# A two-layer hybrid decoder trunk on one core: its list scheduler gets other priorities, another order of tiles and chunks, and other places for the modulation weights in the weight stream

## The chip, the cores and the metric

The kernel runs on one core of a Trainium2 chip. The metric is the device time of one execution in microseconds (us), lower is better. Times are medians of several executions. One further execution was recorded with the hardware profiler, and every duration below comes from that record.

The engines are called as the profile calls them: PE is the matrix unit (its weight loads are listed apart as PEld), DVE the vector engine, ACT the scalar engine, POOL the general one, SP the one that issues most DMAs. Each engine works through its own instructions strictly in the order in which the program gives them; between engines only semaphores set the order.

## What is computed

```python
for l in range(2):
    shift, scale, gate = split(c @ w_ada[l] + b_ada[l], 3)         # adaLN, from one row c
    u = x * (1 + scale) + shift                                    # x is 256 x 1024
    h = u @ w_in[l]                                                # 1024 -> 4032 columns, cut among groups
    o = concat[DSA(4 heads), FoX(6 heads), NSA(6 heads)]           # three kinds of attention
    x = LayerNorm(ALPHA * x + (1 + gate) * ((o * silu(h["gate"])) @ w_out[l]))
```

- **DSA** scores all earlier tokens with a small indexer (8 heads of 32), keeps the 64 best of each row (top-k) and attends to those alone.
- **FoX** is causal attention with a decay that is summed over the tokens.
- **NSA** adds up a compressed, a selected and a windowed branch, each weighted by a gate. With 256 tokens the selected and the windowed branch are both plain causal attention here.

All inputs are float32.

## The kernel before, in words

**Matmuls.** A float32 product of the big projections is made of three passes over reduced floats: each weight piece is cast to a high part (ACT, L516, `wh`) and the remainder is taken by a subtraction (DVE, L534, `wl`); the function `mm3` (L549 to L551) then issues high x high, low x high and high x low. Every weight piece of 512 KB therefore costs a DMA (`raw`), a cast on ACT, a subtraction on DVE, and matmuls. Six `raw` buffers and five `wh` buffers exist.

**Modulation.** The adaLN product `c @ w_ada` is a row times a matrix and is done on DVE: one `scalar_tensor_tensor` with a row sum for each 128 x 1024 piece (L583), 24 pieces for each layer. Such a piece also goes through a `raw` buffer. Its key in the stream is `("ada", layer, j, h)`; h = 0, 1 are scale and shift, needed before the layer starts, h = 2 is the gate, needed at its end.

**Stages of a layer.** (1) Four *chunks* A, B, C, D of about 450 to 512 columns each are projected with tokens on the partitions, for two token halves t = 0, 1: A holds the indexer's queries and keys, B the DSA queries and keys, C the NSA keys, D the NSA queries; the values are spread over all four. After a chunk ACT copies it out (`chunk`), DVE rotates it (rope, L641 to L644), PE transposes it (L655) and ACT copies the transposes. (2) Sixteen *tiles* of 128 columns are projected with columns on the partitions (24 matmuls each): tiles 0 and 1 feed the compressed branch, tiles 2 to 7 are key and query of the three FoX pairs, tiles 8 to 15 are the eight blocks of the output gate. (3) Among the tiles run 11 *pair steps* of attention (two heads at a time: 3 NSA pairs twice, 3 FoX, 2 DSA). Each is a chain over all engines: scores on PE (L722, with L727, L730 or L732 for decay and masks), row maxima on DVE (L677), exponentials on ACT (L681), reciprocal sums on DVE (L667, L668, L670), normalisation on ACT (L694), transposes on PE (L704), a copy on ACT (L708), values on PE (L753), and a copy of the result on ACT (L975). (4) Block i of the output gate times block i of the attention result gives `mH`, `mL` (L1136 to L1141). (5) The output projection takes four pieces for each of two column halves; piece q needs gate blocks 2q and 2q+1. Then residual, LayerNorm, and for layer 0 the next layer's `u` (L1379, L1389, L1403, `uL` L1407) and the affine part of the LayerNorm on x itself (L1430).

DSA's mask comes from the top-k: eight rounds of a maximum and a replacement on DVE (L925, L926) for each token half, after the indexer (L906, L911, L886).

**What sets the order.** Nothing of this is written out by hand. Each piece of work is a generator that asks for an engine and a modelled duration, and a list scheduler (class `Order`) emits instructions in the order of its own modelled clock. On each engine it takes, of what is ready, the task with the lowest priority number. Two things steer it, and both lie in the table `PR` (L364): the priority numbers (`nsa0`, `dsa1`, `fox1` and so on; the last digit is the layer), and the lists that write the weight stream:

```python
        for c in PR["cord"]:
            chunk(c, l)
...
        a, b = PR["ada_at"]
        extra += [(a + b * j, [("ada", 1, j, h) for h in range(2)]) for j in range(8)]
...
        for i in range(16):
            tiles(l, pr("tord", l)[i])
```

`ada_at = (a, b)` puts the pieces of step j of the next layer's scale and shift behind the stream position a + b*j, counted in tiles. SP issues the stream in this order, each DMA as soon as a `raw` buffer is given back. `acc` is the number of PSUM banks that projections may hold, and `aff` the priority of the affine step L1430.

Of the kernel before, what the change touches and what calls it, by code (L numbers as in the profile page):

```python
# [179 lines left out]
def stream_order():  # L180
    o = []

    def chunk(c, l):
        o.extend((c, l, q) for q in range(4))
# [10 lines left out]
    for l in range(DEPTH):  # L195
# [10 lines left out]
        else:  # L206
            for c in PR["cord"]:
                chunk(c, l)
        extra = []
        if l == 0:  # L210
            a, b = PR["ada_at"]
            extra += [(a + b * j, [("ada", 1, j, h) for h in range(2)]) for j in range(8)]
        a, b = PR["adag_at"][l]
        extra += [(a + b * j, [("ada", l, 2 * j + i, 2) for i in range(2)]) for j in range(4)]
# [18 lines left out]
class Order:  # L233
# [38 lines left out]
    def _unblock(self):  # L272
        moved = True
        while moved:
            moved = False
            for t in sorted(self.tasks, key=self._key):
# [6 lines left out]
                elif r[0] == "R":  # L283
# [3 lines left out]
                    if cls in ("s", "pt", "o", "ms", "ad"):  # L287
                        side = sum(self.used.get((tag, c), 0) for c in ("s", "pt", "o", "ms", "ad"))
                        if side + n > PR["side"]:
                            continue  # L290
# [19 lines left out]
    def run(self):  # L310
        while True:
            self._unblock()
            best = None
            for e in "PAVG":
                cand = [(t["ready"] + self.LAT[e], t) for t in self.tasks if t["req"][0] == e]
                if not cand:
                    continue
                first = max(self.free_at[e], min(r for r, _ in cand))
                r, t = min((z for z in cand if z[0] <= first + (PR["tol"] if self._key(z[1])[0] <= -2 else 0.02)),
                           key=lambda z: self._key(z[1]))  # L320
# [14 lines left out]
def pr(name, l):  # L335
    return PR.get(f"{name}{l}", PR.get(name))

# [23 lines left out]


RW = [6, 5]
PR = dict(zn='VV', upart=4, ul='VVVV', nrm='AAAA', cord='ABDC', t1q=0, cuts=(0, 512, 1024), oq=(0, 1, 2, 3), tord=(0, 1, 2, 3, 4, 5, 6, 7, 8, 9, 10, 11, 12, 13, 14, 15), gpp=(0, 1), res=-3.5, warm=10, tol=0.1, ada_at=(12, 0.25), adag_at=((0, 0.5), (11, 1)), ow=(512, 256), aff=0, tw=512, nact=((0, 0), (1, 0), (0, 1), (1, 1)), pro='', gp0=(0, 1), gp1=(0, 1), acc=4, s=2, pt=1, o=3, ms=3, side=8, topk=3, idx=2, dec=0.5, cmp=1.2, nsa=1.6, dsa=1.7, fox=1.8, gate=4, gate1=6, ada=6, main=10, ev=0, split=4, nahead=2, acc1=1.5, cmp1=3, dec0=1.45, nsa1=1.6, topk1=6, nsa0=1.3, dec1=0.5, idx1=0.3, tord1=(2, 3, 4, 5, 6, 7, 0, 1, 8, 9, 10, 11, 12, 13, 14, 15), dsa0=1.4, oq0=(1, 0, 2, 3), cmp0=1.2, fox1=1.5, dsa1=1.7, fox0=1.1, oq1=(1, 2, 3, 0), topk0=3, tord0=(0, 1, 2, 3, 4, 5, 6, 7, 8, 9, 10, 11, 12, 13, 14, 15), idx0=2, nrm1='AAAA', nrm0='AAAA', t1q0=0, t1q1=0)  # L364


@with_exitstack
# [1117 lines left out]
```

## Time and profile before

| | us |
|---|---|
| median of 3 runs | 391.98 (390.94 to 393.09) |
| the profiled execution | 391.34 |
| its span (first to last instruction) | 389.6 |

| stage, by the stream of PE's work | from, us | to, us |
|---|---|---|
| layer 0: chunks with the modulation | 0 | 61 |
| layer 0: ropes, first indexer and NSA scores | 61 | 80 |
| layer 0: tiles and pairs | 80 | 177 |
| layer 0: output projection | 177 | 198 |
| LayerNorm, next `u`, first chunk of layer 1 | 198 | 217 |
| layer 1: rest of the chunks | 217 | 262 |
| layer 1: tiles and pairs | 262 | 362 |
| layer 1: output projection | 362 | 380 |
| last LayerNorm and output | 380 | 389.6 |

A row of the stage view gives a stretch of time, its length, then for PE, PEld, DVE, ACT and POOL the busy time in it with the number of instructions, then PE's granted clock as a share of full speed, the DMA engines' busy share and GB/s. A row of the timeline gives start and duration in us, engine, line, operation, output<-input, shapes, a count where equal instructions are merged, and in brackets the idle time of that engine just before and who ended it.

### The profile page before, as it was taken

Reading aid. Unit: us, or ns where it says so; the run is one execution under the profiler, and the core shown is the slowest. Engines: PE = TensorE matmul, PEld = TensorE weight load, DVE = VectorE, ACT = ScalarE, POOL = GpSimd, SP = SyncE. Lnnn points to the kernel's source line nnn. Section 1 sums busy time; section 2 is a strip of 40 time slices with the busy share of each in tenths; the row PEclk is TensorE's granted clock in tenths of the full one; section 3 lists DMA queues with packets and bytes.
Section 4 is the critical chain, followed back from the end, with each engine's and each line's share of the span. In section 5 each row is a group of like instructions: output and inputs, shape, how many; then the busy total and the mean of one; then the engine's idle time right before and its main releaser. Section 6 shows DMA issues by size and latency. Waiting matters only on the chain.

```text
span 389.6 us, 6872 instructions
## 1 busy us (share of the span) xinstructions
PE 352.2 (90%) x2430; PEld 284.8 (73%) x2430; DVE 314.6 (81%) x766; ACT 252.6 (65%) x664; POOL 8.1 (2%) x14
## 2 busy tenths in 40 slices
PE   5899999799999998589977999999999999997990
PEld 1687788588886786377956768878888898864790
DVE  5798879998989998978899889999565688553766
ACT  3564458676996868773385656556998646987520
POOL 2000000000000000000000000000000000000014
PEclk9899999999999999979988999999999999998996
DMA  7999997638425658796644554563355695110002
GB/s 228 411 408 397 360 352 305 217 110 303 130 64 177 194 177 297 245 315 209 216 133 172 145 174 115 163 209 108 110 142 187 170 407 179 48 63 0 1 2 108
DMA packets 22074, 75.47 MB, mean 194 GB/s; under 512 B 2964, under 2 KB 3096, under 8 KB 21912
## 3 DMA queue, kind: packets, MB, share of 16 engines
q1 hardware_dynamic: 21752, 74.75, 57.1%
q8 instruction: 19, 0.31, 0.3%
q10 hardware_dynamic: 288, 0.29, 0.2%
q14 instruction: 15, 0.12, 0.1%
HBM read 73.98 MB, written 1.05 MB: 193 GB/s over the span
## 4 chain that ended last, share of the span: by engine, by line
PE 49%; DVE 26%; DMA 12%; ACT 8%; issue 4%; DVEq 0%; SPq 0%; ACTq 0%
DMA raw<-in_wst_dram 12%; PE b L549 11%; PE b L551 11%; PE b L550 10%; DVE wl L534 6%; PE b L722 4%; PE b L753 3%; PE b L704 3%; DVE raw L583 2%; DVE iacc L926 2%; DVE iacc L886 2%; ACT wh L516 2%; ACT p L694 2%; DVE m L925 2%; DVE roped L641 1%
## 5 line engine op out<-in xcount | busy, mean ns | idle before, releaser
L516 ACT CAST wh<-raw 128x1024 fp32r<-128x1024 f32 (+2 forms) x81 | 83.3, 1030 | 55.7 <-DMA raw<-in_wst_dram 28.4
L534 DVE TENSOR_TENSOR wl<-raw,wh 128x1024 fp32r<-128x1024 f32 (+2 forms) x81 | 96.2, 1193 | 13.7 <-ACT wh L516 12.9
L549 PE MATMUL b<-uH,wh 128*128 128x256 f32 x256 | 77.4, 302 | 0.0
L551 PE MATMUL b<-uH,wl 128*128 128x256 f32 x256 | 72.9, 285 | 0.2 <-DVE wl L534 0.2
L550 PE MATMUL b<-uL,wh 128*128 128x256 f32 x256 | 72.7, 284 | 0.0
L583 DVE SCALAR_TENSOR_TENSOR raw<-raw,cbc 128x1024 f32<-128x1024 f32 x48 | 58.0, 1218 | 4.3 <-DMA raw<-in_wst_dram 4.0
L549 PE MATMUL b<-wh,uH 128*128 128x512 f32 (+1 forms) x128 | 52.4, 410 | 3.0 <-ACT uH L1359 2.3
L551 PE MATMUL b<-wh,uL 128*128 128x512 f32 (+1 forms) x128 | 51.5, 402 | 3.3 <-DVE uL L1407 1.6
L549 PEld LDWEIGHTS b<-uH,wh 128*128 128x128 f32 x256 | 49.2, 192 | 2.4 <-issue 1.5
L550 PE MATMUL b<-wl,uH 128*128 128x512 f32 (+1 forms) x128 | 51.0, 398 | 0.0
L551 PEld LDWEIGHTS b<-uH,wl 128*128 128x128 f32 x256 | 49.2, 192 | 0.6 <-DVE wl L534 0.6
L550 PEld LDWEIGHTS b<-uL,wh 128*128 128x128 f32 x256 | 49.3, 193 | 0.1
L681 ACT ACTIVATE p<-b,nmx 128x128 f32<-128x128 f32 x88 | 36.3, 428 | 3.5 <-DVE nmx L677 3.4
L694 ACT ACTIVATE p<-p,rinv 128x128 f32<-128x128 f32 (+1 forms) x88 | 33.8, 451 | 2.8 <-DVE rinv L668 1.4
L551 PEld LDWEIGHTS b<-wh,uL 128*128 128x128 f32 x128 | 25.1, 196 | 10.6 <-DVE uL L1361 3.9
L704 PE MATMUL b<-cf,p 128*128 128x128 f32 x132 | 23.9, 290 | 9.4 <-ACT p L694 9.4
L549 PE MATMUL b<-wh,mH 128*128 128x256 f32 (+1 forms) x96 | 31.9, 332 | 0.5 <-ACT mH L1139 0.5
L551 PE MATMUL b<-wh,mL 128*128 128x256 f32 (+1 forms) x96 | 31.2, 325 | 0.5 <-DVE mL L1141 0.5
L549 PEld LDWEIGHTS b<-wh,uH 128*128 128x128 f32 x128 | 25.2, 197 | 8.8 <-ACT uH L1359 2.8
L550 PE MATMUL b<-wl,mH 128*128 128x256 f32 (+1 forms) x96 | 31.1, 324 | 0.0
L708 ACT COPY pT<-b 128x384 f32<-128x384 f32 x44 | 21.2, 484 | 11.6 <-PE b L704 11.1
L550 PEld LDWEIGHTS b<-wl,uH 128*128 128x128 f32 x128 | 24.9, 194 | 4.1
(174 smaller groups left out, 565.0 us busy)
## 6 DMA issues: line engine op xcount, KB each, us to landing
raw<-in_wst_dram SPq DMA_DIRECT2D x120, 512.0 KB, 4.6
raw<-in_wst_dram SPq DMA_DIRECT2D x7, 480.0 KB, 6.6
lnr<-in_lnrow_dram SPq DMA_DIRECT2D x4, 512.0 KB, 4.9
raw<-in_wst_dram SPq DMA_DIRECT2D x4, 448.0 KB, 4.1
xT_sb<-in_xT_dram SPq DMA_DIRECT2D x4, 256.0 KB, 6.6
x_sb<-in_x_dram SPq DMA_DIRECT2D x1, 1024.0 KB, 7.7
out_dram<-x_sb SPq DMA_DIRECT2D x3, 256.0 KB, 2.2
cf<-in_cst_dram SPq DMA_DIRECT2D x1, 384.0 KB
```

What stands on the lines that cost most here:

```text
L516: A.copy(h[:, :n], loaded[key])
L534: V.tensor_tensor(lo[:, :n], raw, h[:, :n].bitcast(F32), op=ALU.subtract)
L549: T.matmul(o, ah, bh, start=start, stop=False)
L550: T.matmul(o, ah, bl, start=False, stop=False)
L551: T.matmul(o, al, bh, start=False, stop=stop)
L583: V.scalar_tensor_tensor(w, w, 1.0, cbc, op0=ALU.mult, op1=ALU.mult, accum_out=mods[l][:, j, h:h + 1])
L681: A.activation(p_sb[:, P * t:P * t + P * (t + 1)], so[:, P * t:P * t + P * (t + 1)], AF.Exp, bias=nmx[:, t, a:a + 1], accum_out=st[:, t, a ...
L694: A.mul(blk, blk, r[:, t, a:a + 1])
L704: T.transpose(pt[:, i, :], p_sb[:, P * i:P * i + P], ident)
L708: A.copy(pT, pt.rearrange("p a b -> p (a b)"))
L722: T.matmul(sp[a][:, P * t:P * t + nk], qT[r, t * P:(t + 1) * P], kT[r, :nk], start=True, stop=False, skip_group_check=True)
L753: T.matmul(O[64 * a:64 * a + 64, P * kt:], vs(a, kt), outs[a][0][:, 256 * kt:256 + 128 * kt], start=(first and kt == 0), stop=(last and kt ...
```

## The change

One line changes, the table `PR`. Its changed entries, one to a line:

```diff
-cord='ABDC'   ada_at=(12, 0.25)   adag_at=((0, 0.5), (11, 1))   aff=0   acc=4
+cord='DCAB'   ada_at=(10, 0.5)    adag_at=((0, 0.5), (8, 1))    aff=0.49   acc=5
...
-dec0=1.45  dsa0=1.4   cmp0=1.2   fox0=1.1
+dec0=0.28  dsa0=0.12  cmp0=1.39  fox0=1.48
-tord0=(0, 1, 2, 3, 4, 5, 6, 7, 8, 9, 10, 11, 12, 13, 14, 15)
+tord0=(0, 1, 3, 4, 5, 6, 7, 8, 9, 10, 11, 12, 13, 2, 14, 15)
...
-nsa1=1.6   topk1=6    idx1=0.3   fox1=1.5   dsa1=1.7   oq1=(1, 2, 3, 0)
+nsa1=5.08  topk1=5.9  idx1=0.64  fox1=1.95  dsa1=4.17  oq1=(1, 3, 2, 0)
-tord1=(2, 3, 4, 5, 6, 7, 0, 1, 8, 9, 10, 11, 12, 13, 14, 15)
+tord1=(2, 4, 6, 7, 0, 1, 8, 9, 5, 3, 14, 10, 12, 13, 11, 15)
```

No operation is added or taken away: the matmuls, DVE and ACT operations and DMAs are the same, in another order. For about the first 80 us the order is the same but for the names of the first tiles. Three places show what moves.

**DVE, layer 0, about the first pieces of layer 1's modulation** (L583; `iacc` with L925 and L926 are top-k rounds, L677 row maxima, L667 and L668 reciprocal sums, L1129 a gate block, L534 a remainder of a weight piece). Before:

```order
L618 TENSOR_TENSOR mod_88<-mod_88,bcol_sb 128x8
L583 SCALAR_TENSOR_TENSOR raw_1428,mod_89<-raw_1428,cbc 128x1024
L667 TENSOR_SCALAR rinv_425_1785<-st_1694 128x4
L668 RECIPROCAL rinv_425_1785<-rinv_425_1785 128x4
L1129 SCALAR_TENSOR_TENSOR sg_1781<-sg_1781,b_1671 128x256
L583 SCALAR_TENSOR_TENSOR raw_1473,mod_89<-raw_1473,cbc 128x1024
L583 SCALAR_TENSOR_TENSOR raw_1541,mod_89<-raw_1541,cbc 128x1024
L583 SCALAR_TENSOR_TENSOR raw_1581,mod_89<-raw_1581,cbc 128x1024
L583 SCALAR_TENSOR_TENSOR raw_1610,mod_89<-raw_1610,cbc 128x1024
```

Now:

```order
L618 TENSOR_TENSOR mod_88<-mod_88,bcol_sb 128x8
L583 SCALAR_TENSOR_TENSOR raw_1222,mod_89<-raw_1222,cbc 128x1024
L677 TENSOR_REDUCE nmx_1644<-b_1630 128x1 x2
L677 TENSOR_REDUCE nmx_1644<-b_1631 128x1 x2
L925 MAX m_409_1691<-iacc_704 128x8
L926 MATCH_REPLACE iacc_704<-m_409_1691,iacc_704 128x128
L583 SCALAR_TENSOR_TENSOR raw_1252,mod_89<-raw_1252,cbc 128x1024
L667 TENSOR_SCALAR rinv_415_1719<-st_1645 128x4
L668 RECIPROCAL rinv_415_1719<-rinv_415_1719 128x4
```

Before, these pieces come in a block behind the last top-k round. Now they start earlier and stand among the last rounds. Further on, the two DSA pairs come before tiles 2, 14 and 15 and the pair FOX0 comes last, where before the DSA pairs came last; and the last of the 16 pieces stands behind the last remainder `mL` that the output projection needs, where before all 16 stood ahead of it.

**DVE, between the layers** (L1263 the normalised x, L1407 `uL`, L1430 the affine step, L641 to L644 the rope of the first chunk's first token half, L534 a weight remainder). Before:

```order
L1263 TENSOR_SCALAR x_sb<-x_sb,mv_2418,tq_2422 128x512
L534 TENSOR_TENSOR wl_2504<-raw_2241,wh_2484 128x1024
L1407 TENSOR_TENSOR uL_2358<-t2k_2495,uH_2357 128x4x128
L1430 TENSOR_TENSOR x_sb<-x_sb,lnr_2451 128x512 x4
L801 TENSOR_SCALAR iw_2454<-chunk_2538 128x8
L802 TENSOR_TENSOR f_2455<-chunk_2538,cf 128x6
L641 TENSOR_TENSOR roped_2546<-chunk_2538,cf 128x288
L642 TENSOR_TENSOR ropet_2547<-chunk_2538,cf 128x9x16
L643 TENSOR_TENSOR ropet_2547<-chunk_2538,cf 128x9x16
L644 TENSOR_TENSOR roped_2546<-roped_2546,ropet_2547 128x288
L806 COPY ik_617_2552<-roped_2546 128x128
L1407 TENSOR_TENSOR uL_2358<-t2k_2524,uH_2357 128x4x128
```

Now:

```order
L1263 TENSOR_SCALAR x_sb<-x_sb,mv_2425,tq_2429 128x512
L1407 TENSOR_TENSOR uL_2358<-t2k_2422,uH_2357 128x4x128
L534 TENSOR_TENSOR wl_2494<-raw_2241,wh_2461 128x1024
L1407 TENSOR_TENSOR uL_2358<-t2k_2460,uH_2357 128x4x128
L1407 TENSOR_TENSOR uL_2358<-t2k_2511,uH_2357 128x4x128
L1430 TENSOR_TENSOR x_sb<-x_sb,lnr_2466 128x512 x2
L641 TENSOR_TENSOR roped_2548<-chunk_2538,cf 128x384
L642 TENSOR_TENSOR ropet_2549<-chunk_2538,cf 128x6x32
L643 TENSOR_TENSOR ropet_2549<-chunk_2538,cf 128x6x32
L644 TENSOR_TENSOR roped_2548<-roped_2548,ropet_2549 128x384
L1430 TENSOR_TENSOR x_sb<-x_sb,lnr_2466 128x512 x4
```

All parts of `uL` now stand ahead of the affine step and the rope. On PE the transposes of that rope (L655), which stood ahead of all matmuls of the first chunk's second token half, now stand behind half of them.

**PE, end of layer 1's tiles: the pair DSA0** (L704 its transposes, one row for each head; L753 the values; L549 to L551 weights). Before, with the output projection's first half as the only filler:

```order
L753 MATMUL b_4286<-pT_4254,vall_2457 64x128
L753 MATMUL b_4286<-pT_4265,vall_2457 64x128
L704 MATMUL b_4302<-cf,p_4261 128x128 x3
L704 MATMUL b_4309<-cf,p_4268 128x128 x3
L549 MATMUL b_4134<-wh_3969,mH_3979 128x512
L550 MATMUL b_4134<-wl_3981,mH_3979 128x512
L551 MATMUL b_4134<-wh_3969,mL_3980 128x512
```

Now, inside tile 11, with tile 15 behind it:

```order
L551 MATMUL b_4172<-uH_2357,wl_3833 128x256
L549 MATMUL b_4172<-uH_2357,wh_3812 128x256
L550 MATMUL b_4172<-uL_2358,wh_3812 128x256
L551 MATMUL b_4172<-uH_2357,wl_3833 128x256
L704 MATMUL b_4228<-cf,p_4149 128x128 x3
L549 MATMUL b_4172<-uH_2357,wh_3812 128x256
L550 MATMUL b_4172<-uL_2358,wh_3812 128x256
L551 MATMUL b_4172<-uH_2357,wl_3833 128x256
```

Before, PE's last tile matmul of layer 1 came ahead of the transposes of four of the five last pairs (FOX1, FOX2, DSA0, DSA1). Now only DSA1's stand behind it; between the scores of DSA0 and its first transposes lie 36 tile matmuls, for DSA1 there are 48. At the start of the tiles the opposite holds: chunks A and B come last, so the indexer, all 16 top-k rounds and the DSA rope stand, on DVE, behind the other chunks, where before 12 of the 16 rounds came ahead of the first NSA pair's row maxima. On DVE the order there is now: rope of B for both token halves (L641 to L644, L828, twice), six steps of the indexer (L886, two over 256 and four over 128 columns), one weight remainder (L534), then the first row maxima (L677).

More of the change, by code (lines that the diff above doesn't have):

```diff
@@ L363 @@
 RW = [6, 5]
-PR = dict(zn='VV', upart=4, ul='VVVV', nrm='AAAA', cord='ABDC', t1q=0, cuts=(0, 512, 1024), oq=(0, 1, 2, 3), tord=(0, 1, 2, 3, 4, 5, 6, 7, 8, 9, 10, 11, 12, 13, 14, 15), gpp=(0, 1), res=-3.5, warm=10, tol=0.1, ada_at=(12, 0.25), adag_at=((0, 0.5), (11, 1)), ow=(512, 256), aff=0, tw=512, nact=((0, 0), (1, 0), (0, 1), (1, 1)), pro='', gp0=(0, 1), gp1=(0, 1), acc=4, s=2, pt=1, o=3, ms=3, side=8, topk=3, idx=2, dec=0.5, cmp=1.2, nsa=1.6, dsa=1.7, fox=1.8, gate=4, gate1=6, ada=6, main=10, ev=0, split=4, nahead=2, acc1=1.5, cmp1=3, dec0=1.45, nsa1=1.6, topk1=6, nsa0=1.3, dec1=0.5, idx1=0.3, tord1=(2, 3, 4, 5, 6, 7, 0, 1, 8, 9, 10, 11, 12, 13, 14, 15), dsa0=1.4, oq0=(1, 0, 2, 3), cmp0=1.2, fox1=1.5, dsa1=1.7, fox0=1.1, oq1=(1, 2, 3, 0), topk0=3, tord0=(0, 1, 2, 3, 4, 5, 6, 7, 8, 9, 10, 11, 12, 13, 14, 15), idx0=2, nrm1='AAAA', nrm0='AAAA', t1q0=0, t1q1=0)
+PR = dict(zn='VV', upart=4, ul='VVVV', nrm='AAAA', cord='DCAB', t1q=0, cuts=(0, 512, 1024), oq=(0, 1, 2, 3), tord=(0, 1, 2, 3, 4, 5, 6, 7, 8, 9, 10, 11, 12, 13, 14, 15), gpp=(0, 1), res=-3.5, warm=10, tol=0.1, ada_at=(10, 0.5), adag_at=((0, 0.5), (8, 1)), ow=(512, 256), aff=0.49, tw=512, nact=((0, 0), (1, 0), (0, 1), (1, 1)), pro='', gp0=(0, 1), gp1=(0, 1), acc=5, s=2, pt=1, o=3, ms=3, side=8, topk=3, idx=2, dec=0.5, cmp=1.2, nsa=1.6, dsa=1.7, fox=1.8, gate=4, gate1=6, ada=6, main=10, ev=0, split=4, nahead=2, acc1=1.5, cmp1=3, dec0=0.28, nsa1=5.08, topk1=5.9, nsa0=1.3, dec1=0.5, idx1=0.64, tord1=(2, 4, 6, 7, 0, 1, 8, 9, 5, 3, 14, 10, 12, 13, 11, 15), dsa0=0.12, oq0=(1, 0, 2, 3), cmp0=1.39, fox1=1.95, dsa1=4.17, fox0=1.48, oq1=(1, 3, 2, 0), topk0=3, tord0=(0, 1, 3, 4, 5, 6, 7, 8, 9, 10, 11, 12, 13, 2, 14, 15), idx0=2, nrm1='AAAA', nrm0='AAAA', t1q0=0, t1q1=0)
 @with_exitstack
```

## The prediction

> **What bounds the kernel now.** I read the stage view first, then the timeline around the three places where PE stops, then the rows by line for durations.
>
> ```profile
> core 0: us, PE busy (x) PEld busy (x) DVE busy (x) ACT busy (x) POOL busy (x), PEclk, DMA share, GB/s
> ...
> 80.00:150.00 70.00, 68.76 (x570) 55.37 (x569) 63.60 (x193) 54.27 (x166) 0.00 (x0) 1.00 0.57 182
> 150.00:177.00 27.00, 19.57 (x125) 14.42 (x125) 24.17 (x51) 20.76 (x54) 0.00 (x0) 0.87 0.82 274
> 177.00:198.00 21.00, 20.70 (x138) 19.03 (x139) 17.69 (x35) 8.84 (x15) 0.00 (x0) 1.00 0.52 173
> 198.00:217.00 19.00, 14.40 (x55) 10.56 (x54) 17.05 (x34) 12.40 (x31) 0.00 (x0) 0.82 0.50 155
> 217.00:262.00 45.00, 44.30 (x232) 35.14 (x231) 41.89 (x106) 27.47 (x64) 0.00 (x0) 1.00 0.57 169
> 262.00:300.00 38.00, 37.78 (x317) 31.54 (x317) 27.23 (x80) 31.68 (x101) 0.00 (x0) 1.00 0.45 134
> 300.00:338.00 38.00, 38.00 (x365) 34.47 (x362) 27.23 (x67) 25.35 (x62) 0.00 (x0) 1.00 0.59 207
> 338.00:362.00 24.00, 20.75 (x130) 12.91 (x128) 10.04 (x32) 19.24 (x63) 0.00 (x0) 0.93 0.14 45
> ```
>
> The reader is to see three things. In layer 0's tiles (80 to 177) DVE is busy 63.60 + 24.17 = 87.8 of 97 us: that stage is DVE's. In layer 1's tiles (262 to 338) PE is never free while DVE and ACT have room. And PE stops in three places, which are also the rows with a granted clock below 1.00: 150 to 177, 198 to 217, 338 to 362.
>
> The first stop, at the end of layer 0:
>
> ```profile
> 164.24 1.05 ACT L516 CAST wh<-raw 128x1024 fp32r<-128x1024 f32 x1 [0.54 <-DMA raw<-in_wst_dram]
> ...
> 165.65 0.48 PE L704 MATMUL b<-cf,p 128*128 128x128 f32 x1 [3.31 <-ACT p L694]
> ...
> 167.92 0.69 PE L704 MATMUL b<-cf,p 128*128 128x128 f32 x2 [1.80 <-ACT p L694]
> ...
> 176.82 0.75 DVE L1141 TENSOR_TENSOR mL<-sg,mH 128x256 fp32r<-128x256 f32 x2
> ```
>
> The DSA pair's normalisation waits on ACT behind a cast that waits for its DMA, and PE, with nothing else in its queue, waits 3.31 and 1.80 us for it. But this stop isn't what the stage costs: the output projection can only go on after the last `mL` at 176.82, at the end of DVE's own queue.
>
> **The change, part by part.** The sum is made against the profiled execution, 391.34 us, of which 389.6 us are the span. The median shown is 391.98 us, 0.64 above, about what single runs differ by.
>
> *Layer 0, tiles and pairs.* Durations first:
>
> ```profile
> L534 DVE TENSOR_TENSOR wl<-raw,wh 128x1024 fp32r<-128x1024 f32 x68 | 82.7, 1220 | 13.7 <-ACT wh L516 12.9
> ...
> L583 DVE SCALAR_TENSOR_TENSOR raw<-raw,cbc 128x1024 f32<-128x1024 f32 x48 | 58.0, 1218 | 4.3 <-DMA raw<-in_wst_dram 4.0
> ```
>
> ```profile
> 338.90 0.39 PE L549 MATMUL b<-wh,mH 128*128 128x512 f32 x1
> 339.13 0.40 PE L550 MATMUL b<-wl,mH 128*128 128x512 f32 x1
> ```
>
> ```profile
> raw<-in_wst_dram SPq DMA_DIRECT2D x120, 512.0 KB, 4.6
> ```
>
> Since DVE's work is unchanged, moving DSA forward can't give more here than DVE's idle time, 97 - 87.8 = 9.2 us, however good PE's order becomes. Two gains are firm. One modulation piece (1.22 us) now stands behind the last `mL`; DVE's idle time in 177 to 198, 21 - 17.69 = 3.3 us, hides it there. And the last `mL` are now those of FOX0 and tile 15, needed by the third piece of the output projection, where before DSA's were needed by the second: six matmuls at 0.23 us, 1.4 us, move ahead of the wait. Of the 9.2 us I take 1.5. More is doubtful, because the moved pieces hand back the buffers for tiles 13, 2, 14 and 15 and for the first output piece one by one: between a piece and the remainder of the tile that its buffer then takes stand about 5.6 to 6 us of DVE work, and landing plus cast take 4.6 + 1.05 = 5.65 us. If each of these five waits misses by as much as the ACT cast at 164.24 did (0.54), 2.7 us come back; if twice that, 5.4. Term: -4 us, between +3 and -11.
>
> *Between the layers.*
>
> ```profile
> 207.52 2.74 DVE L1430 TENSOR_TENSOR x_sb<-x_sb,lnr 128x512 f32<-128x512 f32 x4
> ```
>
> ```profile
> 209.31 0.40 PE L551 MATMUL b<-wh,uL 128*128 128x512 f32 x1
> 211.79 0.44 PE L655 MATMUL b<-cf,roped 128*128 128x128 f32 x2 [2.08 <-DVE roped L644]
> ...
> 212.54 0.63 PE L550 MATMUL b<-wl,uH 128*128 128x512 f32 x1
> ```
>
> PE stands 2.08 us before the rope's transposes, then runs matmuls of 0.63 us in place of 0.40. Now half of the second token half's matmuls come ahead of these transposes, and `uL` no longer waits behind the affine step (2.74 us). Against that, PE has one more batch of transposes ahead of the first chunk and D's rope is wider than A's. The wait of 2.08 us is filled or stands later; I take -1.5, between -3.5 (wait and slow matmuls both gone) and +2 (the same wait again).
>
> *Start of layer 1's tiles: a new wait.* B's rope is now ahead of the first NSA pair on DVE, and so are six indexer steps.
>
> ```profile
> 231.83 1.00 DVE L886 SCALAR_TENSOR_TENSOR iacc<-t2k,iw,iacc 128x256 f32<-128x256 f32 x2
> ```
>
> ```profile
> 234.61 0.48 DVE L641 TENSOR_TENSOR roped<-chunk,cf 128x320 f32<-128x320 f32 x1
> ...
> 236.27 0.48 DVE L641 TENSOR_TENSOR roped<-chunk,cf 128x320 f32<-128x320 f32 x1
> ```
>
> ```profile
> 287.57 1.15 DVE L677 TENSOR_REDUCE nmx<-b 128x1 f32<-128x128 f32 x4 [0.39 <-PE b L732]
> ```
>
> ```profile
> 267.22 0.37 ACT L681 ACTIVATE p<-b,nmx 128x128 f32<-128x128 f32 x1 [2.21 <-DVE nmx L677]
> ...
> 269.11 1.05 ACT L516 CAST wh<-raw 128x1024 fp32r<-128x1024 f32 x1
> ```
>
> ```profile
> 284.87 0.28 PE L549 MATMUL b<-uH,wh 128*128 128x256 f32 x1
> 284.99 0.28 PE L550 MATMUL b<-uL,wh 128*128 128x256 f32 x1
> ```
>
> DVE: two ropes 2 x 1.66 (236.27 - 234.61), two indexer steps 1.00, four of half the width at most as much each, so up to 2, one remainder 1.22, the maxima 1.15: 8.7 us; then exponentials 1.9 us (267.22 to 269.11) before the pair can be normalised and transposed, 10.6 us and more. PE has in the same time 60 tile matmuls at 0.12 = 7.2 us and a few small groups. Behind the waiting transposes stand all tiles. So PE waits some 3.5 us in all, at B's transposes and at the first NSA pair's. Bounds: 0 if the small groups fill it, 8.7 if none of these DVE rows is hidden. Term: +3.5.
>
> *Layer 1, the last five pairs.*
>
> ```profile
> 349.18 1.07 PE L753 MATMUL b<-pT,vall 128*64 128x256 f32 x8
> ...
> 352.06 1.17 PE L704 MATMUL b<-cf,p 128*128 128x128 f32 x5 [0.63 <-ACT p L694]
> ...
> 361.99 0.50 PE L549 MATMUL b<-wh,mH 128*128 128x512 f32 x1 [0.46 <-ACT mH L1139]
> ```
>
> In 338 to 362 weights load for 12.91 us; in the stretch before, at 34.47 of 38 us, this takes 14.2 us. So 9.8 us are waiting. Now the same pairs have tiles between scores and transposes. What stays is DSA1's own chain: before, 12.8 us from its scores (349.18) to the matmul that needs its `mL` (361.99), with almost nothing between. Now 48 tile matmuls (5.8 us), 18 of the output projection (4.1 us) and DSA0's values (1.07) fill 11 us, while ACT has two casts (2.1 us) more within the chain. That leaves 12.8 + 2.1 - 11, about 4 us less what of the casts falls into gaps: I take 3. Term: 3 - 9.8 = -7 us (rounded), between -9.8 and -2; -2 if ACT, busy 19.24 of these 24 us, stays the chain. That ACT has 12.7 us free in 300 to 338, where its work now goes, speaks against that end.
>
> *Between these two:* the top-k moves into the pairs.
>
> ```profile
> L925 DVE MAX8 m<-iacc 128x8 f32<-128x256 f32 x16 | 6.7, 419 | 0.0
> ...
> L926 DVE MATCH_REPLACE8 iacc<-m,iacc 128x256 f32<-128x256 f32 x16 | 6.5, 409 | 0.0
> ```
>
> Twelve rounds of at most 0.83 us, 10 us, come to a stretch where DVE is busy 27.23 + 27.23 + 10.04 = 64.5 of 100 us. They fit: I count 0, and what it costs if they stand ahead of a pair's maxima is the second rival. The last projection and the last LayerNorm keep their order.
>
> Sum: -4 - 1.5 + 3.5 - 7 = -9, and 391.34 - 9 = **382.3 us**.
>
> One rule is to be weighed at the three stops. The rows show granted clocks of 0.87, 0.82 and 0.93; at half speed that is 7.0, 6.8 and 3.4 us, and PE loses half of it, 8.6 us. The Trainium skill, "TensorE: Matmul & The Clock Gate", section "What's actually happening", says that the clock falls to half after about one idle window of 3.4 us, and that windows run freely. The trace agrees in the amounts (3.4 us or multiples). But a wait of 2.08 us was followed by a slow stretch too, so shorter waits than a window do not save the clock for certain. If by that rule all three slow stretches went, the sum would be lower by their part that isn't in the terms, about 1.7 us in layer 1's first chunk: 380.6.
>
> **The rivals.**
>
> *PE closes up in all of layer 1.* From 217 to 362 weights load for 35.14 + 31.54 + 34.47 + 12.91 = 114.1 us. At the density of 300 to 338 (0.907) this takes 125.8 us, not 145: 19.2 us less, 372.1 us. For it: DVE's 41.89 of 45 in 217 to 262 is relieved of the top-k. Against it: groups of short matmuls load less densely whatever waits. Chance 0.14. The Trainium skill ("Perfetto Trace Analysis", section "Identifying the Most-Contended Engine") reads PE's headroom so, by the share of weight loading and not by matmul busy time; the trace agrees that busy time hides it (PE 44.30 of 45 with 35.14 loading).
>
> *Slower: softmax steps wait behind the top-k.* DVE runs in order. If a top-k round, a remainder or a gate piece stands ahead of a pair's maxima and again ahead of its reciprocal, each of the 11 pairs can come up to 0.83 + 1.22 us late at PE. It decides from 9 / 11 = 0.8 us for each pair on, where the whole gain is gone; at 1.4 us it costs 15.4, 397.7 us. For it: all 16 rounds now lie among the six NSA steps. Against: DVE's 35 us of room, and in layer 0, where rounds lay among the pairs already, PE's gaps were short until 160. Chance 0.08.
>
> *No change.* Layer 0 is DVE's and gives only its buffer waits back (0), the boundary waits again (0), the new wait is whole (+8.7), the tail gains 7: 393.0 us, or with the two firm gains 390.4. For it: 87.8 of 97. Chance 0.12.
>
> **How the numbers follow.** The forecast, each term near its value, has 0.66 and spans 375 to 389: the firm parts stay, and the four open terms seldom fall to one side together. 382.3 is its time; a median lies 0.6 higher, so I give 382.5. With the rivals the range is 372 to 391.5. A measurement here tells 0.5%, 2 us, from no change. Faster by more than that (under 390): the forecast less a little, the first rival, some of the third, 0.81; within: 0.10; slower: 0.09.
>
> **What would show it.** In the new profile: the waits of L704 for L694 near the end of layer 1 shrink from several us to about 3, and PEclk stays 1.00 there. In layer 0 DVE is busy over 90% up to the last `mL`; if its idle time before L534 there grows past 5 us, the buffer term is wrong. A new wait of L655 for L644, or of L704 for L694, of some us stands at the start of layer 1's tiles. If L681 waits for L677 throughout the NSA steps, the second rival is right. The prediction is wrong if the tail stays: then ACT, not the order on PE, was what ended last.

## The result and the profile after

The changed kernel takes 377.45 us (median of 4 runs, 376.46 to 378.44) against 392.53 us for the kernel before, now over 4 runs (390.94 to 394.65). The ratio is 0.961 with a 95% interval of 0.956 to 0.967: 15 us less. 382.5 us were forecast, with a range of 372 to 391.5. The profiled execution took 378.44 us with a span of 376.7 us, 12.9 us less than the span before.

The chain of work that ended last, first before, then of the changed kernel, each as the page has it by engine:

```profile
PE 49%; DVE 26%; DMA 12%; ACT 8%; issue 4%; DVEq 0%; SPq 0%; ACTq 0%
```

```profile
PE 67%; DMA 14%; DVE 13%; ACT 2%; issue 2%; SPq 0%; DVEq 0%; ACTq 0%
```

PE's own work is now two thirds of the chain; DVE and ACT, on which PE used to wait in turn, have gone from 34% to 15%.

To see where this came from, both spans are cut at the same instructions, not at the same times: the first tile matmul of layer 0, its first attention scores (L722), the last `mL` of layer 0 (L1141), the last matmul of its output projection, the first tile matmul of layer 1, and the last matmul of its output projection. The stage view with these cuts, before:

```profile
57.66:80.34 22.68, 19.59 (x186) 16.19 (x184) 21.78 (x68) 16.81 (x60) 0.00 (x0) 1.00 0.67 238
80.34:177.57 97.23, 88.27 (x692) 70.06 (x691) 88.00 (x244) 74.75 (x216) 0.00 (x0) 0.96 0.65 209
177.57:197.86 20.29, 20.27 (x136) 18.60 (x136) 16.99 (x33) 8.70 (x15) 0.00 (x0) 1.00 0.51 169
197.86:258.84 60.98, 56.38 (x267) 43.56 (x266) 55.98 (x132) 38.01 (x89) 0.00 (x0) 0.94 0.55 166
258.84:379.64 120.80, 116.64 (x947) 97.68 (x945) 80.55 (x210) 84.96 (x238) 1.38 (x2) 0.99 0.37 120
```

And of the changed kernel:

```profile
57.62:83.28 25.66, 21.79 (x185) 17.96 (x183) 23.63 (x70) 16.85 (x60) 0.00 (x0) 0.87 0.63 213
83.28:175.51 92.23, 87.82 (x698) 71.13 (x697) 85.69 (x240) 74.70 (x216) 0.00 (x0) 0.98 0.66 209
175.51:194.44 18.93, 18.91 (x130) 17.48 (x130) 17.71 (x36) 8.60 (x15) 0.00 (x0) 1.00 0.60 212
194.44:252.24 57.80, 52.98 (x257) 42.33 (x256) 46.59 (x93) 37.16 (x85) 0.00 (x0) 0.97 0.60 187
252.24:366.72 114.48, 114.48 (x957) 97.58 (x956) 89.65 (x248) 85.93 (x243) 1.37 (x2) 1.00 0.39 123
```

| stage | before, us | changed, us | difference | predicted |
|---|---|---|---|---|
| first tile to first scores, layer 0 (order unchanged) | 22.68 | 25.66 | +2.98 | 0 |
| A: first scores to the end of layer 0's projection | 117.52 | 111.16 | -6.36 | -4 |
| B: from there to layer 1's first tile | 60.98 | 57.80 | -3.18 | -1.5 |
| C: layer 1's tiles, pairs and projection | 120.80 | 114.48 | -6.32 | +3.5 - 7 = -3.5 |

These add up to -12.9, the difference of the spans. The first row is not the change's doing (last section). Row C holds a smaller part of that kind: before, PE's clock was at half for a stretch in its tail (0.99 in the row of that stage), and e1 below, with the old order there and no such stretch, took 119.48 us. Against e1, C is 5.0 us shorter. Without both, the spans would differ by some 14.6 us; the medians say 15.1. In C, PE's waits before and after, as the view of waits lists them between the cuts (us in total, times, longest); before:

```profile
PE b L704 <- ACT p L694: 2.8, 5, 0.9
PE b L655 <- DVE roped L644: 0.9, 2, 0.7
PE b L549 <- ACT mH L1139: 0.5, 1, 0.5
```

For the changed kernel this view is empty: from 252 to 367 us PE waits for nothing that lasts long enough to be listed, and its clock is 1.00 throughout. DVE's busy time in B and C shows the top-k rounds that have moved: 55.98 to 46.59 in B, 80.55 to 89.65 in C.

### The profile page after: what moved, and what is told of

Read it like the earlier page. It is cut to its first block, busy times and chain, and to the rows that moved or that the text cites. A ratio compares the mean times of both kernels' runs of the same rounds, so it can differ in the third digit from the quotient of the medians.

```text
span 376.7 us, 6853 instructions
## 1 busy us (share of the span) xinstructions
PE 347.4 (92%) x2430; PEld 285.3 (76%) x2430; DVE 314.1 (83%) x766; ACT 252.6 (67%) x664; POOL 8.1 (2%) x14
## 4 chain that ended last, share of the span: by engine, by line
PE 67%; DMA 14%; DVE 13%; ACT 2%; issue 2%; SPq 0%; DVEq 0%; ACTq 0%
PE b L549 15%; PE b L551 15%; PE b L550 14%; DMA raw<-in_wst_dram 12%; PE b L722 5%; PE b L753 4%; PE b L704 4%; DVE raw L583 3%; DVE wl L534 3%; DMA lnr<-in_lnrow_dram 2%; PE b L732 2%; PE b L655 2%; ACT wh L516 2%; PE b L906 2%; PE b L625 1%
## 5 line engine op out<-in xcount | busy, mean ns | idle before, releaser
L534 DVE TENSOR_TENSOR wl<-raw,wh 128x1024 fp32r<-128x1024 f32 (+2 forms) x81 | 96.0, 1193 | 14.0 <-ACT wh L516 12.9
L549 PE MATMUL b<-uH,wh 128*128 128x256 f32 x256 | 78.2, 305 | 0.0
L551 PE MATMUL b<-uH,wl 128*128 128x256 f32 x256 | 73.5, 287 | 0.4 <-DVE wl L534 0.4
L583 DVE SCALAR_TENSOR_TENSOR raw<-raw,cbc 128x1024 f32<-128x1024 f32 x48 | 58.2, 1217 | 4.2 <-DMA raw<-in_wst_dram 4.0
L549 PE MATMUL b<-wh,uH 128*128 128x512 f32 (+1 forms) x128 | 51.8, 405 | 2.0 <-ACT uH L1359 2.0
L551 PE MATMUL b<-wh,uL 128*128 128x512 f32 (+1 forms) x128 | 50.8, 397 | 1.6 <-DVE uL L1361 1.6
L549 PEld LDWEIGHTS b<-uH,wh 128*128 128x128 f32 x256 | 50.0, 195 | 2.0 <-issue 1.3
L551 PEld LDWEIGHTS b<-uH,wl 128*128 128x128 f32 x256 | 49.8, 195 | 0.6 <-DVE wl L534 0.6
L694 ACT ACTIVATE p<-p,rinv 128x128 f32<-128x128 f32 (+1 forms) x88 | 34.4, 454 | 0.9 <-DVE rinv L670 0.8
L549 PE MATMUL b<-wh,mH 128*128 128x256 f32 (+1 forms) x96 | 31.2, 325 | 0.0
L551 PE MATMUL b<-wh,mL 128*128 128x256 f32 (+1 forms) x96 | 30.7, 320 | 0.4 <-DVE mL L1141 0.4
L551 PEld LDWEIGHTS b<-wh,uL 128*128 128x128 f32 x128 | 24.7, 193 | 8.2 <-DVE uL L1361 3.7
L549 PEld LDWEIGHTS b<-wh,uH 128*128 128x128 f32 x128 | 24.9, 194 | 7.7 <-ACT uH L1359 2.9
L550 PEld LDWEIGHTS b<-wl,uH 128*128 128x128 f32 x128 | 24.7, 193 | 4.1
L708 ACT COPY pT<-b 128x384 f32<-128x384 f32 x44 | 21.2, 484 | 8.1 <-PE b L704 8.1
L704 PE MATMUL b<-cf,p 128*128 128x128 f32 x132 | 23.3, 282 | 2.9 <-ACT p L694 2.8
```

What stands on the lines that cost most here:

```text
L534: V.tensor_tensor(lo[:, :n], raw, h[:, :n].bitcast(F32), op=ALU.subtract)
L549: T.matmul(o, ah, bh, start=start, stop=False)
L550: T.matmul(o, ah, bl, start=False, stop=False)
L551: T.matmul(o, al, bh, start=False, stop=stop)
L583: V.scalar_tensor_tensor(w, w, 1.0, cbc, op0=ALU.mult, op1=ALU.mult, accum_out=mods[l][:, j, h:h + 1])
L694: A.mul(blk, blk, r[:, t, a:a + 1])
```

## The experiments

Single runs differ by a per cent, as much as most of the parts are worth. So each run is read by its stages, which repeat far better: C came out at 114.47 to 114.52 in every run in which layer 1's order was that of the changed kernel.

| run | ratio to before (95%) | A | B | C |
|---|---|---|---|---|
| before | | 117.52 | 60.98 | 120.80 |
| e1 layer 0 alone | 0.984 (0.981 to 0.987) | 110.93 | 61.14 | 119.48 |
| e2 layer 1 alone | 0.994 (0.991 to 0.997) | 117.59 | 61.51 | 116.67 |
| e3 chunk order and affine step alone | 0.993 (0.989 to 0.997) | 117.54 | 58.15 | 120.25 |
| changed | 0.961 (0.956 to 0.967) | 111.16 | 57.80 | 114.48 |
| e4 changed, acc 4 | 0.965 (0.960 to 0.969) | 111.70 | 58.03 | 114.50 |
| e5 changed, old chunk order | 0.976 (0.971 to 0.981) | 110.98 | 62.00 | 116.62 |
| e6 changed, old `ada_at` | 0.958 (0.954 to 0.962) | 111.26 | 57.29 | 114.49 |
| e7 changed, old `tord0` | 0.961 (0.958 to 0.964) | 111.68 | 57.91 | 114.48 |
| e8 changed, old `dsa1` | 0.967 (0.963 to 0.972) | 111.09 | 58.23 | 117.22 |
| e9 changed, old priorities of layer 0 | 0.967 (0.960 to 0.973) | 113.79 | 57.55 | 114.52 |
| e10 changed, old `aff` | 0.960 (0.954 to 0.967) | 113.28 | 58.40 | 114.47 |
| e11 changed, old `tord1` | 0.963 (0.958 to 0.968) | 112.86 | 57.57 | 115.43 |
| e12 changed, chunks DABC | 0.963 (0.958 to 0.969) | 111.07 | 58.66 | 113.75 |

**One set of entries at a time.** e1, the kernel before with layer 0's entries:

```diff
+dec0=0.28 dsa0=0.12 cmp0=1.39 fox0=1.48 ada_at=(10, 0.5)
+tord0=(0, 1, 3, 4, 5, 6, 7, 8, 9, 10, 11, 12, 13, 2, 14, 15)
```

> The kernel before with only the entries of layer 0's tiles and pairs (dec0, dsa0, cmp0, fox0, tord0, ada_at). Measured from the change: the output projection of layer 0 ends 3.4 us earlier (194.4 for 197.9 us). Theory A, each set of entries works alone at its own stage: 3.4 us less than before (ratio 0.991), nothing else moves. Theory B, the sets need each other, here the fifth accumulator (acc=5) that lets a held-back tile stay open: under 1.5 us, or slower. By either, the waits of L704 for L694 between 150 and 177 us (5.9 us before) fall, and DVE's last mL comes 2 us earlier if A holds.

It took 386.92 us against 392.93, 1.6% less. The comparison with e2 is the cleanest, since that run has the old order up to 201 us and the same length of the first stage (23.86 and 23.81 us). A is 110.93 against 117.59: 6.7 us. Theory A holds, and the part is larger than the 3.4 us that the ends of the two projections alone had shown. C, where the order is that of before, is 1.3 us shorter as well: its tail had no slow stretch of the clock in this execution (1.00 for 0.99), although PE's waits there were as long (L704 for L694: 3.0 us, before 2.8).

e2, the kernel before with layer 1's entries:

```diff
+nsa1=5.08 topk1=5.9 idx1=0.64 fox1=1.95 dsa1=4.17 oq1=(1, 3, 2, 0) adag_at=((0, 0.5), (8, 1))
+tord1=(2, 4, 6, 7, 0, 1, 8, 9, 5, 3, 14, 10, 12, 13, 11, 15)
```

> The kernel before with only the entries of layer 1's tiles and pairs (nsa1, topk1, idx1, fox1, dsa1, oq1, tord1, adag_at); the order of the chunks stays ABDC. Measured from the change: from layer 1's first tile to the end of its output projection 114.5 us for 120.8. Theory A: 6.3 us less (ratio 0.984), the waits of L704 for L694 in the tail (2.8 us) and its slow clock gone. Theory A with the predicted price of chunk B coming last (3.5 us): that price isn't paid with ABDC, so 9 to 10 us less (0.975). Theory B, the new priorities fit only the new chunk order: under 3 us.

C fell by 4.1 us, not by 6.3 and not by 9 to 10; against e1's C, which has the old order and no slow stretch either, it is 2.8. So the old chunk order does not save the price that the prediction put on B coming last; on the contrary, something of the gain is missing.

e3, the kernel before with the chunks and the affine step:

```diff
+cord='DCAB' aff=0.49
```

> The kernel before with only the order of the chunks and the affine steps' place (cord DCAB, aff 0.49). Measured from the change: from the end of layer 0's output projection to the last chunk matmul 56.8 us for 60.8. Theory A: 3.9 us less (ratio 0.990), with the wait of L655 for L644 (2.1 us) replaced by one of L1379 for L1263. Theory B: layer 1's pairs, whose priorities (nsa1 1.6) put them ahead at once, now wait for chunk B, so that the gain between the layers goes back in 260 to 300 us: within 1.5 us of before, or slower, with new waits of L704 or L655 there.

B fell by 2.8 us, and C did not grow (120.25 for 120.80). Against e1's 119.48, at the same clock, it is 0.8 us longer, which is what the ten matmuls are worth that have moved behind the cut (below, between the layers). From 258 to 300 us the view lists no wait of PE at all. This already speaks against the new wait at the start of layer 1's tiles. The sets don't simply add up: in B and C together e2 gives 3.6 and e3 3.4 us, and both at once, in the changed kernel, 9.5 (with e1's C in place of that of before: 2.3, 2.1 and 8.2).

e4, the changed kernel with one accumulator less:

```diff
-acc=5
+acc=4
```

> The changed kernel with acc=4 for 5 (one accumulator less that tiles and output pieces may hold), so the three sets of entries of the runs beside it put together. Theory A, sets add up and acc matters little: 12 to 13 us less than before (ratio 0.968), and equal to the sum of the three runs within 2 us. Theory B, acc=5 carries the held-back tiles: 4 to 8 us of the gain go, with PE waiting before the tiles' first matmuls.

Not one row of any engine's order differs between acc=5 and acc=4, so this is the changed kernel a second time: 379.06 us (378.21 to 381.66), all three stages within 0.6 us. The entry does nothing.

**Undoing one entry of the changed kernel.** e5:

```diff
-cord='DCAB'
+cord='ABDC'
```

> The changed kernel with the chunks in the old order (cord ABDC), all else changed. The prediction's term for layer 1's tiles said that B coming last costs 3.5 us there; then from layer 1's first tile to its last projection matmul this run takes about 111 us for 114.5, and 3 us more between the layers (61 for 57.8): no difference in all. The runs so far say the opposite, that B last costs nothing and even helps the new priorities: 116.7 us in layer 1 and 61 between, about 5 us more than the changed kernel (ratio to before 0.978).

383.85 us: B and C each go back, by 4.2 and 2.1 us, as the runs before had said and the prediction's term had not. PE's waits in its layer 1 are those that DCAB is rid of:

```profile
PE b L655 <- DVE roped L644: 0.9, 2, 0.7
PE b L549 <- ACT mH L1139: 0.5, 1, 0.5
```

They are 1.4 of the 2.1 us.

e6 and e7, two entries of layer 0:

```diff
-ada_at=(10, 0.5)
+ada_at=(12, 0.25)
```

> The changed kernel with layer 1's modulation pieces in their old place (ada_at (12, 0.25)). The prediction counted 1.2 us for the one piece that now stands behind the last mL. If that is all this entry does: 1.2 us more from layer 0's first NSA scores to the end of its output projection (112.4 for 111.2). If the pieces spread among the tiles also fill DVE's idle time or spread the transfers: 3 to 5 us more (114 to 116), with DVE's idle time before the last mL back from 6.5 to 9 us. If the later start is a help: under 0.5.

```diff
-tord0=(0, 1, 3, 4, 5, 6, 7, 8, 9, 10, 11, 12, 13, 2, 14, 15)
+tord0=(0, 1, 2, 3, 4, 5, 6, 7, 8, 9, 10, 11, 12, 13, 14, 15)
```

> The changed kernel with layer 0's tiles in number order (tile 2 third and not fourteenth). If the held-back tile 2 is what PE works on while the pairs' softmax runs: 3 to 5 us more in layer 0 (114 to 116 from first NSA scores to the end of the projection, for 111.2). If the pairs' new priorities alone do it: within 1 us.

Neither costs more than 0.5 us. In both orders the last modulation piece still stands behind the last `mL`, so the 1.2 us of the prediction's step weren't undone by e6 and hang on something else.

e8, the DSA pairs of layer 1:

```diff
-dsa1=4.17
+dsa1=1.7
```

> The changed kernel with layer 1's DSA pairs at their old priority (dsa1 1.7 for 4.17): they come last again or later than now. The prediction took 3 us as what DSA1's own chain still makes PE wait. By the new trace nothing waits, since small groups and the projection's first half fill it. If the fill behind DSA1's scores is what counts: the waits of L704 for L694 in the tail come back with 1 to 3 us and a slow stretch of the clock, 2 to 5 us more in layer 1 (116.5 to 119.5 for 114.5). If the order of tiles alone (tord1) does it: within 1 us of 114.5.

C grows by 2.7 us. The wait that comes back isn't the transposes' (L704) that was expected, but the projection's for the last pair's `mH`:

```profile
PE b L549 <- ACT mH L1139: 1.5, 1, 1.5
PE b L753 <- ACT pT L708: 0.2, 1, 0.2
```

No slow stretch of the clock followed (1.00 in 340 to 360 us). The expectation also had the order wrong. A lower number is taken earlier: the DSA pairs (L730 is their mask) now come before the FoX pairs, and the pair that comes last is a FoX pair (L727 is its decay).

```profile
307.84 0.49 PE L722 MATMUL b<-q,q 64*128 64x128 f32 x4
308.26 0.29 PE L730 MATMUL b<-dmask,cb 128*128 128x128 bf16 x2
...
337.20 0.49 PE L722 MATMUL b<-f,f 64*128 64x128 f32 x4
337.62 0.23 PE L727 MATMUL b<-cum,cb 96*128 96x128 bf16 x1
```

The last pair's scores begin 85.0 us after the first tile, in the changed kernel 81.4. Behind them stand 12 tile matmuls in place of 48, so less work is left to fill the last pair's chain.

e9, layer 0's priorities:

```diff
-dec0=0.28 dsa0=0.12 cmp0=1.39 fox0=1.48
+dec0=1.45 dsa0=1.4 cmp0=1.2 fox0=1.1
```

> The changed kernel with the priorities of layer 0's groups back (dec0, dsa0, cmp0, fox0), the tile order and all else changed. Neither the modulation's place nor the tile order made more than 0.5 us of layer 0's gain in the runs before. If it is the pairs' priorities: 116 to 117.5 us from first NSA scores to the end of layer 0's projection, for 111.2, with the waits of L704 for L694 back to 5 us or more and DVE's idle time near 9 us. If the entries stand in for each other, so that any of them gives most of the gain: under 113.

113.79 us, between the two expectations: 2.6 us of the 6.4 go back. Of the two signs, DVE's idle time did come back (93.80 - 84.67 = 9.1 us), the waits of L704 for L694 did not (0.9 us). From the last `mL` to the end of the projection it takes 19.99 us for 18.93: two more matmuls lie there, and PE waits 0.48 us for a weight remainder. The rest can't be told from the scatter of A, which e10 and e11 show.

e10 and e11:

```diff
-aff=0.49
+aff=0
```

> The changed kernel with the affine steps' place back (aff 0), chunk D still first. The prediction gave part of its gain between the layers to uL no longer waiting behind the affine step (2.74 us). If so: 1 to 3 us more between the layers (59 to 61 for 57.8) and a longer wait of L655 for L644. If the chunk order alone does it: within 0.5 us of 57.8, with the wait of 4.0 us of L1379 for L1263 as in the changed kernel.

```diff
-tord1=(2, 4, 6, 7, 0, 1, 8, 9, 5, 3, 14, 10, 12, 13, 11, 15)
+tord1=(2, 3, 4, 5, 6, 7, 0, 1, 8, 9, 10, 11, 12, 13, 14, 15)
```

> The changed kernel with layer 1's tiles in their old order. The run with the DSA priority back took 2.7 us more in layer 1, and the new priorities with the old chunk order 2.1 more. If the tail's gain needs the tiles that make PE's fill to be those that no pair waits for: 2 to 5 us more in layer 1 (116.5 to 119.5 for 114.5). If the priorities alone carry it: within 1 us.

e10: B is 58.40 us, 0.6 more, with the same wait of 4.0 us (L1379 for L1263) and a lower clock (0.94 for 0.97). The chunk order makes the gain between the layers, not the affine step's place. e11: C is 0.95 us longer, so the tile order is the smaller part of the tail's gain. Both have layer 0 exactly as the changed kernel, and yet A took 113.28 and 112.86 us. The timeline of e11 shows where:

```profile
159.85 1.04 ACT L516 CAST wh<-raw 128x1024 fp32r<-128x1024 f32 x1 [3.03 <-DMA raw<-in_wst_dram]
160.80 0.85 ACT L708 COPY pT<-b 128x384 f32<-128x384 f32 x2
160.93 1.23 DVE L534 TENSOR_TENSOR wl<-raw,wh 128x1024 fp32r<-128x1024 f32 x1 [2.53 <-ACT wh L516]
161.33 1.03 PE L753 MATMUL b<-pT,vall 128*64 128x256 f32 x6 [3.32 <-ACT pT L708]
```

The same place in the changed kernel:

```profile
158.97 1.05 ACT L516 CAST wh<-raw 128x1024 fp32r<-128x1024 f32 x1 [0.79 <-DMA raw<-in_wst_dram]
159.92 0.85 ACT L708 COPY pT<-b 128x384 f32<-128x384 f32 x2
```

A weight piece landed late, ACT stood 3.03 us in place of 0.79 before its cast, and the pair's copy (L708), for which PE waited, stood behind the cast in ACT's queue. In e10 PE's wait there was 2.1 us, and the clock of the stage up to the last `mL` 0.96 for 0.98. The same order so gives 110.9 to 113.3 us; the old order gave 117.5 to 117.6 three times.

e12, the chunk order once more:

```diff
-cord='DCAB'
+cord='DABC'
```

> The changed kernel with the chunks in the order DABC: D first as now, but A and B ahead of C, so that indexer, top-k and DSA rope start earlier. If the gain between the layers comes from D being first: 57 to 58.5 us there, one wait of 4.0 us. If A and B coming late costs nothing in layer 1, as the runs so far say: layer 1 at 114 to 116.5. If it cost the predicted 3.5 us: layer 1 at 111 to 112, and this is the fastest kernel, some 3 us ahead of the changed one.

B and C together take 172.41 us, those of the changed kernel 172.28: no difference. With D first, it doesn't matter whether A and B come second and third or last, and 379.53 us (377.94 to 380.03) is no faster kernel. Against e5 only D has moved (ABDC and DABC), with the same number of PE's matmuls on either side of the cut: B 3.3 us less, C 2.9 us less. No run beat the changed kernel beyond its interval.

## Why the prediction was right, and where it was not

The direction and the range were right; the gain was forecast at 9 us and is 15. Step by step:

**Layer 0 (-4 predicted, -6.4 measured): the firm steps right, one size and one reading off.** DVE stayed busy for over 90% of the time before the last `mL`, 88.00 of 97.23 and then 85.69 of 92.23 us. The firm steps came as counted. The piece of the modulation stands behind the last `mL` at 174.76:

```profile
174.76 0.75 DVE L1141 TENSOR_TENSOR mL<-sg,mH 128x256 fp32r<-128x256 f32 x2
175.43 1.22 DVE L534 TENSOR_TENSOR wl<-raw,wh 128x1024 fp32r<-128x1024 f32 x1
176.56 1.22 DVE L583 SCALAR_TENSOR_TENSOR raw<-raw,cbc 128x1024 f32<-128x1024 f32 x1
```

The six matmuls of the output projection that moved ahead of the wait show in the projection's stage (x136 to x130): 20.29 to 18.93, 1.36 us for 1.4. What was mis-sized is the idle time. Of DVE's 9.2 us I took 1.5; it fell to 92.23 - 85.69 = 6.5 in the profiled run, and between e2 and e1, with equal first stages, from 97.29 - 86.89 = 10.4 to 92.00 - 85.65 = 6.35, 4 us. The five buffer waits that I held against more do exist, but as scatter and not as a fixed price: DVE waited 2.2 us for casts there in the changed kernel, 0.7 in e1 with the same order, 0.9 before. Which entry gives the 4 us is open: undone one at a time, the modulation's place, the tile order and the priorities each cost 2.6 us or less, with a scatter of 2.4. They may stand in for each other; no run undid two of them at once.

The reading that failed is that the stop at 164 to 168 us "isn't what the stage costs". The chain that ended last in the kernel before goes through it on its way to the last `mL`:

```profile
160.16 1.14 DVE raw L583 x2
161.33 5.06 DMA raw<-in_wst_dram
166.42 1.04 ACT wh L516
167.92 0.69 PE b L704 x2
```

A modulation piece gives its buffer back, a weight piece lands, ACT casts it, and only then come the pair's normalisation and PE's transposes. PE's waits for L694 went from 6.6 to 2.8 us, DVE's waits for ACT's part of the gate blocks (L1129 for L1127) from 3.6 to 1.2, while the clock of the stage rose from 0.96 to 0.98. Nor is the whole stage DVE's: in the changed kernel the chain lies on PE alone from 83 to 140 us, and on DVE and the weight pieces from there on.

**Between the layers (-1.5 predicted, -3.2 measured).** The wait of 2.08 us before the rope's transposes was filled, down to 0.8. But I didn't see that another would take its place: with D first, the transposes of the next part of x (L1379) follow each other, and nothing stands before the last of them.

```profile
194.56 0.60 PE L1379 MATMUL b<-cf,x_sb 128*128 128x128 f32 x4
199.21 0.80 PE L1379 MATMUL b<-cf,x_sb 128*128 128x128 f32 x4 [4.05 <-DVE x_sb L1263]
199.66 0.72 PE L549 MATMUL b<-wh,uH 128*128 128x448 f32 x1
200.18 0.57 PE L550 MATMUL b<-wl,uH 128*128 128x448 f32 x1
```

So PE waits as long as before, 4.0 + 0.8 against 2.1 + 1.6 + 0.7 + 0.2 = 4.6 us. The gain that I can place is in the clock and the cut. Mostly in one piece, the waits were followed by one slow stretch, in two pieces by two (0.94 of 60.98 and 0.97 of 57.80 us, so at half clock 7.3 and 3.5 us); PE's loss from them falls by up to 1.9. Ten of PE's matmuls now lie behind the cut (x267 and x257, then x947 and x957), which e12 and the changed kernel put at 0.8 us. Some 0.7 us I can't place. It may be as much as 1.8 us, since e10, with the clock at 0.94 again, still took only 58.40 us. My reason that `uL` no longer waits behind the affine step counted for little: e10 lost 0.6 us at most by it.

**The new wait at the start of layer 1's tiles (+3.5 predicted, none measured): this step failed.** The chain on DVE was there and as long as worked out. From B's rope to the end of the first pair's maxima:

```profile
250.87 0.48 DVE L641 TENSOR_TENSOR roped<-chunk,cf 128x320 f32<-128x320 f32 x1
...
257.54 1.14 DVE L677 TENSOR_REDUCE nmx<-b 128x1 f32<-128x128 f32 x4
```

That is 258.68 - 250.87 = 7.8 us for the 8.7 that were summed. Wrong was what I set against it on PE: 7.2 us of tile matmuls and "a few small groups" that I gave no time. The chain begins at 250.87, while PE still works at the last chunk (its last matmul starts at 251.28). From the first tile matmul (252.24) to the first pair's transposes (264.02) PE then works for 11.8 us without a listed wait: the 60 tile matmuls make 7.2 of them, and the transposes of B's two ropes, an indexer group and the scores of two pairs with their masks the other 4.6. The margin is small, since ACT begins to normalise the first pair only at 262.47. e3 (no wait listed there), e5 (C longer without B last) and e12 (A and B earlier, nothing gained) agree.

**The tail of layer 1 (-7 predicted; for all of C -6.3 measured, -5.0 against e1).** Right in place; that the size is near is luck, since two errors partly cancel. The 9.8 us that I called waiting came from the density of weight loading in 300 to 338; the waits proper there were 2.8 + 0.5 = 3.3 us, with a slow stretch of the clock that cost about 1.3 more (e1), and the rest was the lower density of short groups, which they keep wherever they stand (97.58 of 114.48 us in C now, 0.85, for 0.91 in that dense stretch). On the other side, the 3 us left for DSA1's own chain came to nothing. It took about 13 us, where I had worked out 12.8 + 2.1: its scores end at 335.3, and the last `mH` stands at 348.4.

```profile
335.83 1.14 DVE L677 TENSOR_REDUCE nmx<-b 128x1 f32<-128x128 f32 x4
...
346.24 0.87 PE L753 MATMUL b<-pT,vall 128*64 128x256 f32 x8
...
348.02 0.41 ACT L1139 CAST mH<-sg 128x256 fp32r<-128x256 f32 x1 [0.49 <-DVE sg L1136]
```

But the transposes of DSA0 and DSA1 and DSA1's own values fill PE as well, beside the tiles, DSA0's values and the projection that I had counted. PE's idle time in all of C went from 119.48 - 115.11 = 4.4 us (e1) to nothing, most of the 5.0.

Tile matmuls behind the last scores, my reason for the term, are not what it takes. In e11 none stand there, as in the kernel before, and PE waits only 0.5 us. What e11 keeps is the distance between the pairs: the scores of DSA0 and DSA1 begin 79.3 and 86.6 us after the first tile, in the kernel before 85.5 and 88.7, in the changed kernel 75.5 and 81.4. That this distance counts is read from the orders; no run changes it alone. e8 puts 2.7 us of the tail on the DSA priority, e11 1.0 on the tile order, e5 2.1 on the chunk order. That the chunk order acts on layer 1's tiles and tail at all I hadn't seen; 1.4 of its us are the two waits shown for e5, and what makes the rest stays open.

**The rivals.** PE closing up in all of layer 1 (372.1) did not happen; the density of short groups held, as argued against it. Softmax steps behind the top-k: the exponentials' row of the changed kernel's page,

```profile
L681 ACT ACTIVATE p<-b,nmx 128x128 f32<-128x128 f32 x88 | 36.3, 428 | 1.4 <-DVE nmx L677 1.4
```

has 1.4 us of waiting for the maxima in the whole span, where it was 3.4, although all of layer 1's top-k now lies in C; refuted. No change: two of its conditions failed, a layer 0 that gains nothing and the new wait in full.

One small sum is off too: 382.3 with 0.64 us more for a median is 382.9, not 382.5.

## What to carry to other kernels

When steps move to fill a wait, count everything that stands between the two ends on the waiting engine, small groups too, and from when the chain on the other engine really starts: both errors here made a wait where there was none. Cut two traces at the same instructions and not at the same times; one stage here repeated to 0.05 us where whole runs scatter by 1%, and showed entries of 1 us, while another scattered by 2.4 us and hid them. Which chunk comes first was worth more than which came last: with the one first that the first attention pairs take their queries from, 3 us went between the layers and 3 us more in the layer behind (e12 against e5; why the layer behind gains is open).

## What the runs showed of the hardware

In the clock records of these traces the granted clock falls to half in pieces of 3.41 us, and whether a wait sets one off depends on more than its length. From first tile to first scores of layer 0, where the order is the same, the stage rows above show 22.68 us at a clock of 1.00 and 25.66 us at 0.87. The longest wait there is the same: 2.2 us once before L655 in both. 1 - 0.87 of 25.66 us is 3.3 us lost, so 6.7 us at half clock: two pieces, none before. Ten of the other runs had one piece and took 23.5 to 24.7 us; e7 and e12 had two and took 24.9 and 24.7. The tail of layer 1 shows the same with shorter waits: before, a piece followed waits of at most 0.9 us each, and in e1, with the same order and waits, none came.

The Trainium skill, "TensorE: Matmul & The Clock Gate", section "What's actually happening", says that the windows of activity run freely, so that it depends on where in a window the work falls; the trace agrees, with 3 us between two executions of one order. It also names idle windows of about 3.4 us; here a longest wait of 2.2 us was enough in every execution but one. So the span of one profiled execution against another's carries such pieces, up to 1.7 us each, that no change of the order made.
